# TensorE in written order through the mixing stage of two transformer blocks

## The chip, the core and the metric

The kernel runs on one core of a Trainium2 chip. The metric is the time of one execution on the device, in microseconds (us). TensorE multiplies matrices, VectorE (DVE in the profile) and ScalarE (ACT) work elementwise, GpSimd (POOL) does a few elementwise steps, and SyncE (SP) issues the transfers of the weights. Each engine takes its instructions from a queue of its own, one after the other, and waits at the head of that queue until what the instruction needs is there.

## The reference, cut to what matters

The reference runs two transformer blocks one after the other on 256 tokens with 2,048 features, all in float32. The change lies in the second block, ahead of its feed-forward part:

```
h = rms_norm(x);  z = h @ w_in                       # 1024 pool columns, 3 x 1024 for r, k, v, and 288 more
d = causal_multiscale_pool(z_pool)                   # windows 2, 4, 8, 16
pool_out = einsum('btgc,gcd->btgd', d, pool_w) * pool_scale
w, a, g = small products of the 288 columns, through tanh and sigmoid
kk = k * k_k / norm per head;  k = k * (1 + (a - 1) * k_a)
for t in range(256):                                 # 16 heads of 64, state S of 64 x 64 per head
    S = S * decay_t + (S @ -kk_t) (kk_t a_t)^T + v_t k_t^T;   y_t = S @ r_t
y = group norm of y per head + (sum of r k r_k) v;  y = y * g
x = x + concat(pool_out, y) @ w_out
```

The kernel computes the loop over t in four chunks of 64 tokens. Inside a chunk the steps become small matrix products and the inverse of a triangular 64 x 64 matrix per head; from chunk to chunk the state S is handed on.

## The kernel before, in words

**Fill: the large products.** A weight matrix is streamed from memory in tiles of 128 x 1024 numbers. `load_w` (line 320) has SyncE issue the transfer (L322), ScalarE round the tile to a high part (L325) and VectorE subtract it to get a low part (L326); raw, high and low tiles have three buffers each. `wide_steps` (line 360) multiplies with the weight as the stationary side: each step is a pair of products, L379 over 512 columns and L381 over 256, and 32 pairs fill one PSUM tile `pp` of 256 features; then a copy on ScalarE (L387) and two VectorE instructions (L388, L390) take the sums out. Sixteen products use up one weight tile. `group_steps` (line 337) has the activations as the stationary side: each step is a triple of products over 512 columns (L351 to L353), and twelve products use up one weight tile. `pp` has two buffers. Both are generators: `wide_steps` yields 1 for a pair and `group_steps` 2 for a triple.

**Steps: the small products of the recurrence.** The 16 heads go in two halves of four tiles (two heads in a tile). For each half: `rwkv_pre` (line 1099) squares k, sums it per head (L1084), takes a reciprocal root on VectorE, spreads it (L1090), builds decayed copies of r, k and kk on ScalarE, VectorE and GpSimd, multiplies them (L1161), masks the products on VectorE (L1162, L1163) and transposes a decayed copy (L1169), two tiles at a time. `inverse16` (line 689) inverts the 16 x 16 blocks: SyncE sends the products to memory and back (L701, L702), VectorE does 15 steps of two instructions (L707, L709), GpSimd one copy, and SyncE sends the result out and back again (L710, L712, L716). `rwkv_values` (L1181 to L1188) lays out v. `inverse64` (line 720) starts on GpSimd (L726) and makes the full inverse by products L735, L742 and L744 with VectorE between them. `rwkv_chunk` (line 1206) runs four times per half: L1210, a copy on ScalarE, L1215 and L1217, a copy on ScalarE, L1225 and L1227, an addition on VectorE to the state that the next chunk reads. `rwkv_post` (line 1234) is the group norm: L1240, L1084 and L1090 again. All these products go to PSUM tiles `ps`, of which there are four.

**What sets the order.** The program is written as one sequence. `run` (line 1332) takes a generator of steps, and after each step pulls as many units of fill as the next entry of the list `after` (line 1321) says; the fill is, in this order, the projections of r and v for the first half, the first half of the pool, k, r and v for the second half, the mixing products of the first pool half, the second pool half, the rows of `w_out` for the first half of the heads, and the mixing products of the second pool half. `need` finishes a projection whatever the entries say. The loop is

```
    for half in range(2):
        pre = [None] * 4
        run(merge(rwkv_pre(half, pre), post() if half else ()))
        run(rwkv_half(half, pre))
    run(rwkv_post(1))
    pull(1000)
```

The program is then scheduled as a whole (`schedule_with_timeline_sim=True`, line 1449): for each engine a scheduler plays a timeline forward and, whenever the engine is free in it, takes of the instructions that are ready in it the one that was written first. So an instruction that isn't ready in that timeline is overtaken by later ones; on the chip the order so found is fixed. Lines 1051 to 1057 (small products of the 288 columns) are written ahead of the loop.

**Ten stretches.** Both orders pass through the same steps, so the stage is cut here by steps, and the fill products of each stretch are counted. "Before" is counted in the trace; "written" follows from the list and the loops (a pair is 2 products, a triple 3, and the last step of a PSUM tile counts 1).

| | from the end of ... | to ... | entries of `after` in it | before: pairs' + triples' products | written |
|---|---|---|---|---|---|
| A | first sums, L1084 | last L1161, half 0 | 43 left of r, then 2, 28, 0, 2, 0, 2, 2, 17, 0 | 223 + 0 | 192 + 0 |
| B | A | first L735 | 2, 0, 2, 25, 2, 4, 3, 3, 43 | 214 + 0 | 168 + 0 |
| C | B | first L1210 | 17, 10, 15, 2, 0 | 32 + 0 | 88 + 0 |
| D | C | last L1227 | 4, 2, 3, 2, 3, 3, 0, 0, 3, 10, 3, 2, 3, 2 | 198 + 0 | 80 + 0 |
| E | D | first L1161, half 1 | 4, 1, 0, 28, 24, 3, 13, 1, 21 | 61 + 0 | 190 + 0 |
| F | E | last L1161 | 4, 2, 0, 2, 2, 17, 2 | 8 + 48 | 24 + 27 |
| G | F | first L735 of half 1 | 2, 0, 4, 19, 3, 3, 1, 1, 45 | 128 + 53 | 70 + 69 |
| H | G | first L1210 of half 1 | 15, 10, 13, 1, 0 | 0 + 44 | 58 + 15 |
| I | H | last L1227 of half 1 | 7, 3, 1, 4, 2, 0, 4, 2, 4, 2, 3, 2, 2, 3 | 16 + 143 | 0 + 63 |
| J | I | the rows of `w_out` for the second half | 3, 0, 23, 16, 1, and the rest | 0 | 16 + 114 |

Of the kernel before, what the change touches and what calls it, by code (L numbers as in the profile page):

```python
# [96 lines left out]
def rounds(gens):  # L97

    gens = list(gens)
    while gens:  # L100
        got = [(g, next(g, gens)) for g in gens]
        got = [(g, n) for g, n in got if n is not gens]
        gens = [g for g, n in got]
        yield sum(n or 0 for g, n in got)


def merge(a, b):

    a, b = iter(a), iter(b)
    for _ in a:  # L110
        yield True
        if next(b, False):
            yield True
    yield from b
# [8 lines left out]
def two_blocks_kernel(ctx: ExitStack, tc: tile.TileContext, I: dict, out: bass.AP):  # L123
# [29 lines left out]
    def c(name, lo=0, hi=128):  # L153
        return tabs[name][lo:hi]
# [4 lines left out]
    def prm(name, i, lo=0, hi=128, n=1):  # L159
        t, o = PROW[name]  # L160
        return PT[t][lo:hi, o + i:o + i + n]
# [23 lines left out]
    def wk(tag, F, dt=F32, bufs=2, p=128):  # L185
        return tm(tag, F, dt, bufs, p, quad)

    def psum(F=512, p=128):
        shape = [p] + (list(F) if isinstance(F, (tuple, list)) else [F])
        return ps.tile(shape, F32, tag="ps", name=nm("ps"))  # L190
# [47 lines left out]
    def rsqrt(dst, src, t):  # L238

        ts(out=t.bitcast(I32), in0=src.bitcast(I32), scalar1=1, scalar2=None, op0=ALU.logical_shift_right)  # L240
        ts(out=dst.bitcast(I32), in0=t.bitcast(I32), scalar1=-1, scalar2=0x5F3759DF, op0=ALU.mult, op1=ALU.add)
        for f in (3.0, 12.0, 768.0):
            tt(out=t, in0=dst, in1=dst, op=ALU.mult)
            tt(out=t, in0=t, in1=src, op=ALU.mult)
            stt(dst, t, -f, dst, ALU.add, ALU.mult)
        ts(out=dst, in0=dst, scalar1=-1.0 / 8192, scalar2=None, op0=ALU.mult)

    def tiny(shape):
        return tm("tiny", shape, bufs=8)
# [149 lines left out]
    class Fill:  # L399
# [8 lines left out]
        def pull(self, n):  # L408
            self.owed += n
            while self.todo and self.owed > 0:  # L410
                got = next(self.todo[0], None)
                if got is None:
                    self.todo.pop(0)
                else:
                    self.owed -= got
            if not self.todo:
                self.owed = 0.0
# [11 lines left out]
                self.pull(n)  # L429

    fills = Fill()

    def split(hi, lo, src):
        act(hi, src, AF.Copy)
        tt(out=lo, in0=src, in1=hi.bitcast(F32), op=ALU.subtract)
# [637 lines left out]
    def need(j, half):  # L1073

        for _ in rkvs[j, half]:
            pass
# [3 lines left out]
    def head_sums(p, m, src):  # L1080

        for i in range(2):
            o = 4 * m + 2 * i
            mm(p[:, o:o + 2], src[:, i * 128:(i + 1) * 128], two, start=(m == i == 0), stop=True, skip_group_check=True)  # L1084

    def head_spread(p, f, start=True):

        for i in range(2):
            for j, s in enumerate((LO, HI)):
                mm(p[s, i * 128:(i + 1) * 128], f[:, 2 * i + j:2 * i + j + 1].to_broadcast([128, 64]), ident,  # L1090
                   start=(start and i == 0), stop=True, skip_group_check=True)
# [7 lines left out]
    def rwkv_pre(half, pre):  # L1099

        hs = range(4 * half, 4 * half + 4)

        need(1, half)
        sq = [wk("GB", (4, 128), bufs=4).rearrange("p a b -> p (a b)")[:, :T] for _ in hs]
        for m, h in enumerate(hs):
            act(sq[m], rkv[1, half, m], AF.Square, scale=prm("k_k_2", h))
        yield True
        p = psum()
        for m in range(4):
            head_sums(p, m, sq[m])  # L1110
        n, rn = tiny(16), tiny(16)
        ts(out=n, in0=p[:, :16], scalar1=1e-24, scalar2=None, op0=ALU.max)
        rsqrt(rn, n, tiny(16))
        yield True
        need(0, half)
        for m in (0, 2):
            sp = psum((2, T))
            for i in range(2):
                head_spread(sp[:, i], rn[:, 4 * (m + i):4 * (m + i) + 4], start=(i == 0))
            for _ in rounds([rwkv_pre1(half, m + i, sp[:, i], pre) for i in range(2)]):  # L1120
                yield True
# [53 lines left out]
    def rwkv_values(half, m, SV):  # L1175

        r, k, v = (rkv[j, half, m] for j in range(3))
        t = tm("cva", T, bufs=3)
        stt(t, r, prm("r_k_2", 4 * half + m), k, ALU.mult, ALU.mult)
        pb = psum()  # L1180
        mm(pb[:, :T], c("bones"), t, start=True, stop=True)  # L1181

        pv = psum((4, 128))
        nc.tensor.transpose(pv[:, 1], v[:, 0:128], ident)
        nc.tensor.transpose(pv[:, 2], v[:, 64:192], ident)
        nc.tensor.transpose(pv[:, 3], v[:, 128:256], ident)
        mm(pv[64:128, 0, 0:64], v[0:64, 0:64], ident[0:64, 0:64], start=False, stop=True, skip_group_check=True)
        mm(pv[0:64, 0, 64:128], v[64:128, 192:256], ident[64:128, 64:128], start=False, stop=True, skip_group_check=True)  # L1188
        SV[m] = S = wk("SV", (4, 2, 64), bufs=4)
        act(S[HI, :, 0], pv[HI, :, 0:64], AF.Copy)  # L1190
        act(S[LO, 0:3, 1], pv[LO, 1:4, 64:128], AF.Copy)
        act(S[LO, 3, 1], pv[LO, 0, 64:128], AF.Copy)
        nc.gpsimd.memset(S[LO, 0, 0], 0.0)
        nc.gpsimd.memset(S[HI, 0, 1], 0.0)
        tt(out=v, in0=v, in1=pb[:, :T], op=ALU.mult)
        yield True

    def rwkv_inverse(m, pre, Z):

        GB = pre[2]  # L1200
        X, pd = yield from inverse64([GB[:, i] for i in range(4)], Z[:, m], ("X", "BK")[m % 2])
        for s in (LO, HI):
            tt(out=GB[s, :, s], in0=X[s, :, 1], in1=pd[s, :, 1], op=ALU.subtract)
        yield
# [29 lines left out]
    def rwkv_post(half):  # L1234
        hs = range(4 * half, 4 * half + 4)

        sq = [wk("BT", (4, 128), bufs=4).rearrange("p a b -> p (a b)")[:, :T] for _ in hs]
        for m, h in enumerate(hs):
            pm = psum()
            mm(pm[:, :T], c("bones"), sw[h], start=True, stop=True)  # L1240
            stt(sw[h], pm[:, :T], -1.0 / 64, sw[h], ALU.mult, ALU.add)
            act(sq[m], sw[h], AF.Square)
        yield True
        p = psum()
        for m in range(4):
            head_sums(p, m, sq[m])
        n, rn = tiny(16), tiny(16)
        ts(out=n, in0=p[:, :16], scalar1=1.0 / 64, scalar2=64e-5, op0=ALU.mult, op1=ALU.add)
        rsqrt(rn, n, tiny(16))
        yield True  # L1250
        for m, h in enumerate(hs):
            y = sw[h]
            if m % 2 == 0:
                sp = psum((2, T))
                for i in range(2):
                    head_spread(sp[:, i], rn[:, 4 * (m + i):4 * (m + i) + 4], start=(i == 0))
            stt(y, y, prm("gn_g_2", h), sp[:, m % 2], ALU.mult, ALU.mult)
            stt(y, y, prm("gn_b_2", h), rkv[2, half, m], ALU.add, ALU.add)
            tt(out=y, in0=y, in1=gg[h], op=ALU.mult)
            rwh.append(wk(f"aa{h}", T, F32R, bufs=1))  # L1260
            rwl.append(wk(f"gg{h}", T, F32R, bufs=1))
            split(rwh[h], rwl[h], y)
        yield True

    def rwkv_half(half, pre):

        Z = inverse16([p[2] for p in pre], 4)
        yield True
        SV = [None] * 4
        for m in range(4):  # L1270
            need(2, half)
            yield from rwkv_values(half, m, SV)
        for _ in rounds([rwkv_inverse(m, pre[m], Z) for m in range(4)]):
            yield True
        for j in range(4):
            for _ in rounds([rwkv_chunk(j, pre[m], SV[m], sw[4 * half + m]) for m in range(4)]):
                yield True
# [54 lines left out]
    def run(steps):  # L1332
        for _ in steps:
            pull(next(after))

    def post():
        yield from rwkv_post(0)
        fill.insert(max(1, len(fill) - 1), residual_steps(I["w_out_2"][0], 8, list(zip(rwh[:4], rwl[:4]))))

    for half in range(2):  # L1340
        pre = [None] * 4
        run(merge(rwkv_pre(half, pre), post() if half else ()))
        run(rwkv_half(half, pre))
    run(rwkv_post(1))
    pull(1000)
    n5 = Norm(lambda k: prm("mlp_norm_2", k))
    residual(I["w_out_2"][0], 12, list(zip(rwh[4:], rwl[4:])), n5)
    r5 = spread(n5.finish())
# [104 lines left out]
```

## Time and profile before

| | |
|---|---|
| time, median of 3 runs | 2849.91 us (2837.38 to 2856.08) |
| the profiled execution: its time; its span | 2833.93 us; 2832.2 us |
| TensorE, VectorE, ScalarE, GpSimd busy in the span | 2767.0, 1856.2, 1397.8, 159.2 us |
| mean granted TensorE clock | 0.985 |
| the ten stretches A to J | 1595.85 to 1976.00 us of the span, 380.15 us |
| in them, TensorE busy; VectorE busy | 354.25; 292.26 us |

Times in the profile count from the start of the span. [...] The busy time of TensorE has modelled ends, so that a row of busy time can hide gaps of less than 0.15 us. Counts of a stretch include an instruction that crosses its edge.

### The profile page before, as it was taken

How to read it: one execution, taken by the hardware profiler on the slowest of the kernel's cores; microseconds unless marked ns; L12 is line 12 of the kernel's file. 1: busy time of each engine (PE TensorE's matmuls, PEld its weight loads, DVE VectorE, ACT ScalarE, POOL GpSimd, SP SyncE). 2: the span in 40 equal slices, each digit the busy share in tenths (PEclk: the TensorE clock that was granted, in tenths of full speed). 3: DMA queues.
4: the chain of work that ended last, by engine and by line, in shares of the span. 5: the costliest groups of instructions: out<-in, count | busy, mean ns of one | idle time of the engine just before them, and what ended most of it. 6: DMA issues, size and time to landing. Idle time of an engine off the chain costs nothing.

```text
span 2832.2 us, 40520 instructions
## 1 busy us (share of the span) xinstructions
PE 2767.0 (98%) x15538; PEld 2329.3 (82%) x15538; DVE 1856.2 (66%) x2908; ACT 1397.8 (49%) x2088; POOL 159.2 (6%) x217
## 2 busy tenths in 40 slices
PE   9999989999999999999999999899999999999997
PEld 7888877888888888888887777777888888888886
DVE  7786766555577755775666696876765655656565
ACT  6664545444455544554455544334543444434454
POOL 0003200000000000000001120230000000000001
PEclk9999999999999999999999999899999999999999
DMA  7565644666566656655656363253566666666554
GB/s 218 165 177 150 173 137 119 185 187 186 186 186 189 191 189 188 187 187 190 203 188 183 101 159 108 77 142 105 176 192 193 187 191 191 188 193 204 186 186 149
DMA packets 398200, 487.94 MB, mean 172 GB/s; under 512 B 38426, under 2 KB 283173, under 8 KB 398005
## 3 DMA queue, kind: packets, MB, share of 16 engines
q1 hardware_dynamic: 397221, 482.93, 56.5%
q8 instruction: 122, 2.00, 0.3%
q10 hardware_dynamic: 608, 2.11, 0.2%
q0 software_dynamic: 176, 0.30, 0.1%
q14 instruction: 73, 0.60, 0.1%
HBM read 479.25 MB, written 6.03 MB: 171 GB/s over the span
## 4 chain that ended last, share of the span: by engine, by line
PE 91%; DVE 4%; DMA 2%; ACT 1%; issue 1%; POOL 1%; SPq 0%; DVEq 0%; POOLq 0%; ACTq 0%
PE pp L379 28%; PE pp L381 15%; PE pp L351 14%; PE pp L352 14%; PE pp L353 14%; DVE lo L326 1%; PE ps L267 1%; DMA Z<-s 0%; PE ps L742 0%; DMA raw<-in_w_down_dram 0%; PE ps L1215 0%; PE ps L735 0%; DVE L L1149 0%; PE ps L1217 0%; POOL X L726 0%
## 5 line engine op out<-in xcount | busy, mean ns | idle before, releaser
L326 DVE TENSOR_TENSOR lo<-raw,hi 128x1024 fp32r<-128x1024 f32 x902 | 1108.7, 1229 | 808.0 <-ACT hi L325 784.1
L325 ACT ACTIVATE hi<-raw 128x1024 fp32r<-128x1024 f32 x902 | 953.6, 1057 | 1195.1 <-PE pp L352 554.1
L379 PE MATMUL pp<-xhl,hi 128*128 128x512 f32 x3648 | 1291.7, 397 | 2.1 <-DVE z L388 2.1
L381 PE MATMUL pp<-xhl,lo 128*128 128x256 f32 x3648 | 1030.9, 283 | 2.3 <-DVE lo L326 2.3
L379 PEld LDWEIGHTS pp<-xhl,hi 128*128 128x128 f32 x3648 | 684.0, 188 | 164.7 <-DVE z L388 2.4
L381 PEld LDWEIGHTS pp<-xhl,lo 128*128 128x128 f32 x3648 | 688.8, 189 | 10.2 <-issue 4.7
L353 PE MATMUL pp<-lo,hid 128*128 128x512 f32 x864 | 338.2, 391 | 0.5 <-DVE lo L326 0.5
L351 PE MATMUL pp<-hi,hid 128*128 128x512 f32 x864 | 338.3, 392 | 0.0
L352 PE MATMUL pp<-hi,hid 128*128 128x512 f32 x864 | 337.6, 391 | 0.0
L353 PE MATMUL pp<-lo,xhl 128*128 128x512 f32 (+1 forms) x544 | 206.4, 379 | 0.0
L352 PE MATMUL pp<-hi,xhl 128*128 128x512 f32 (+1 forms) x544 | 206.3, 379 | 0.0
L351 PE MATMUL pp<-hi,xhl 128*128 128x512 f32 (+1 forms) x544 | 206.2, 379 | 0.0
L353 PEld LDWEIGHTS pp<-lo,hid 128*128 128x128 f32 x864 | 162.3, 188 | 35.9 <-DVE lo L326 1.0
L351 PEld LDWEIGHTS pp<-hi,hid 128*128 128x128 f32 x864 | 162.3, 188 | 35.1 <-ACT hi L325 0.3
L352 PEld LDWEIGHTS pp<-hi,hid 128*128 128x128 f32 x864 | 162.4, 188 | 34.3
L351 PEld LDWEIGHTS pp<-hi,xhl 128*128 128x128 f32 x544 | 102.6, 189 | 18.7
L352 PEld LDWEIGHTS pp<-hi,xhl 128*128 128x128 f32 x544 | 102.6, 189 | 18.4
L353 PEld LDWEIGHTS pp<-lo,xhl 128*128 128x128 f32 x544 | 102.5, 188 | 18.3
L933 DVE TENSOR_TENSOR x<-x,pp 128x512 f32<-128x512 f32 x96 | 61.6, 683 | 31.7 <-PE pp L353 31.7
L388 DVE TENSOR_TENSOR z<-pp,z 128x512 f32<-128x512 f32 (+2 forms) x119 | 80.8, 679 | 1.3 <-ACT z L387 1.1
L390 DVE TENSOR_TENSOR z<-z,rstd 128x512 f32<-128x512 f32 x114 | 78.4, 688 | 3.3
L287 POOL TENSOR_TENSOR junk<-x,rows 128x512 f32<-128x512 f32 x8 | 13.4, 1670 | 1110.2 <-ACT junk L284 1110.2
(415 smaller groups left out, 2535.7 us busy)
## 6 DMA issues: line engine op xcount, KB each, us to landing
raw<-in_w_in_dram SPq DMA_DIRECT2D x244, 512.0 KB, 3.6
raw<-in_w_up_dram SPq DMA_DIRECT2D x176, 512.0 KB, 4.4
raw<-in_w_ffn_up_dram SPq DMA_DIRECT2D x128, 512.0 KB, 3.7
raw<-in_w_ffn_down_dram SPq DMA_DIRECT2D x128, 512.0 KB, 4.1
raw<-in_w_down_dram SPq DMA_DIRECT2D x88, 512.0 KB, 3.7
raw<-in_w_out_dram SPq DMA_DIRECT2D x64, 512.0 KB, 3.7
raw<-in_w_ple_gate_dram SPq DMA_DIRECT2D x32, 512.0 KB, 3.9
raw<-in_w_branch_a_dram SPq DMA_DIRECT2D x16, 512.0 KB, 3.7
```

Of the source, the lines that this page charges most:

```text
L267: nc.tensor.transpose(p[:w, m - m0, i * 128:(i + 1) * 128], src[:, i, 128 * m:128 * m + w], ident)
L287: nc.gpsimd.tensor_tensor(out=y, in0=s, in1=self.w2[j], op=ALU.mult)
L325: act(h, r, AF.Copy)
L326: tt(out=l, in0=r, in1=h.bitcast(F32), op=ALU.subtract)
L351: mm(p, xh, h[:, j], start=(k == 0), stop=False, skip_group_check=True)
L352: mm(p, xl, h[:, j], start=False, stop=False, skip_group_check=True)
L353: mm(p, xh, l[:, j], start=False, stop=last, skip_group_check=True)
L379: mm(P[:w, m].rearrange("p a b -> p (a b)"), h[:, j, f], x2.rearrange("p a b -> p (a b)"), start=(k == 0), stop=False, skip_group_check=True)
L381: mm(P[:w, m, 0], l[:, j, f], x2[:, 0], start=False, stop=last, skip_group_check=True)
L388: tt(out=z, in0=P[:w, :nw, 0], in1=z, op=ALU.add)
L390: tt(out=z, in0=z, in1=r()[:w].unsqueeze(1).to_broadcast([w, nw, T]), op=ALU.mult)
L933: tt(out=s, in0=s, in1=p, op=ALU.add)
```

## The change

Both the loop over the halves and the two lines behind it are put into a block in which TensorE's instructions keep the order in which they are written. The order of the other engines and of the transfers is still the scheduler's, which now finds it against that order of TensorE. No instruction is added or taken away.

```
+    def pe_in_order():
+
+        return tc.manual_schedule(engines={mybir.EngineType.PE})
...
-    for half in range(2):
-        pre = [None] * 4
-        run(merge(rwkv_pre(half, pre), post() if half else ()))
-        run(rwkv_half(half, pre))
-    run(rwkv_post(1))
-    pull(1000)
+    with pe_in_order():
+        for half in range(2):
+            pre = [None] * 4
+            run(merge(rwkv_pre(half, pre), post() if half else ()))
+            run(rwkv_half(half, pre))
+        run(rwkv_post(1))
+        pull(1000)
```

## Rows read from the trace of the kernel before

**Rows 1.** The page, part 1: busy time, share of the span, instructions.

```profile
PE 2767.0 (98%) x15538; PEld 2329.3 (82%) x15538; DVE 1856.2 (66%) x2908; ACT 1397.8 (49%) x2088; POOL 159.2 (6%) x217
```

**Rows 2.** Stretches: length, busy (count) of PE, PEld, DVE, ACT, POOL; clock, DMA, GB/s.

```profile
1595.85:1655.30 59.45, 53.48 (x329) 45.25 (x328) 53.22 (x83) 22.58 (x33) 22.07 (x34) 0.94 0.46 130
1655.30:1698.48 43.18, 43.18 (x259) 37.18 (x258) 39.09 (x84) 25.29 (x46) 9.89 (x17) 1.00 0.66 166
1698.48:1717.68 19.20, 17.11 (x352) 14.79 (x352) 14.13 (x22) 3.66 (x4) 4.17 (x5) 1.00 0.36 112
1717.68:1775.51 57.83, 57.83 (x506) 45.68 (x502) 32.58 (x71) 30.24 (x85) 2.02 (x6) 1.00 0.37 106
1775.51:1799.57 24.06, 22.64 (x154) 19.71 (x150) 18.11 (x50) 7.05 (x16) 6.81 (x12) 0.86 0.25 78
1799.57:1837.40 37.83, 29.87 (x145) 24.37 (x146) 37.10 (x63) 14.72 (x24) 11.06 (x18) 0.73 0.25 77
1837.40:1879.21 41.81, 40.76 (x226) 33.67 (x226) 35.68 (x73) 17.46 (x29) 6.39 (x8) 1.00 0.68 172
1879.21:1905.69 26.48, 24.17 (x364) 19.93 (x364) 18.28 (x38) 7.60 (x11) 14.88 (x27) 0.87 0.33 108
1905.69:1964.82 59.13, 57.95 (x472) 43.40 (x468) 37.33 (x79) 30.10 (x86) 0.00 (x0) 1.00 0.40 123
1964.82:1976.00 11.18, 7.26 (x52) 6.62 (x52) 6.73 (x24) 1.28 (x5) 0.00 (x0) 0.61 0.16 47
```

**Rows 3.** The same ten stretches, TensorE's instructions on tile pp alone.

```profile
1595.85:1655.30 59.45, 43.30 (x223) 0.94 0.46 130
1655.30:1698.48 43.18, 39.69 (x214) 1.00 0.66 166
1698.48:1717.68 19.20, 6.67 (x32) 1.00 0.36 112
1717.68:1775.51 57.83, 38.61 (x198) 1.00 0.37 106
1775.51:1799.57 24.06, 14.77 (x61) 0.86 0.25 78
1799.57:1837.40 37.83, 17.15 (x56) 0.73 0.25 77
1837.40:1879.21 41.81, 36.65 (x181) 1.00 0.68 172
1879.21:1905.69 26.48, 12.93 (x44) 0.87 0.33 108
1905.69:1964.82 59.13, 39.38 (x159) 1.00 0.40 123
1964.82:1976.00 11.18, 0.00 (x0) 0.61 0.16 47
```

**Rows 4.** Tile pp on TensorE ahead of the first L1051 product.

```profile
1545.30:1555.19 9.89, 9.89 (x57) 1.00 0.80 248
```

**Rows 5.** Busy time in three spells at the lower clock.

```profile
1646.35:1653.17 6.82, 5.75 (x18) 4.73 (x19) 6.71 (x9) 0.86 (x1) 3.12 (x9) 0.50 0.52 142
1782.88:1789.71 6.83, 6.83 (x25) 6.06 (x25) 4.39 (x23) 0.63 (x1) 0.00 (x0) 0.50 0.23 79
1803.36:1823.84 20.48, 15.79 (x68) 12.93 (x67) 20.16 (x34) 7.08 (x15) 4.55 (x5) 0.50 0.34 104
```

**Rows 6.** TensorE's timeline: start, length, instruction, idle before it and what ended it.

```profile
1702.61 0.68 PE L735 MATMUL ps<-BK,GB 64*64 64x64 f32 x16 [0.72 <-POOL pool L1295]
```

**Rows 7.** Groups by line on VectorE, stretch D: busy us, mean ns, idle before.

```profile
L326 DVE TENSOR_TENSOR lo<-raw,hi 128x1024 fp32r<-128x1024 f32 x13 | 15.9, 1226 | 21.9 <-ACT hi L325 21.7
...
L388 DVE TENSOR_TENSOR z<-pp,z 128x512 f32<-128x512 f32 x4 | 2.8, 692 | 0.1
...
L390 DVE TENSOR_TENSOR z<-z,rstd 128x512 f32<-128x512 f32 x3 | 2.1, 692 | 0.1
```

**Rows 8.** Timeline of SyncE's queue, stretch B: start, length, what it issued.

```profile
1665.59 21.87 SPq L322 DMA_DIRECT2D raw<-in_w_in_dram  x7
```

## The prediction

> **What bounds the kernel now.** I read the page's busy times first: TensorE is busy in 98% of the span, VectorE in 66% [rows 1]. The change touches one part of the span, so I cut that part into the ten stretches of the table above and read each engine's busy time [rows 2]. The reader is to see two kinds of stretch. In A, E, F and J TensorE is idle for 6.0, 1.4, 8.0 and 3.9 us (length less busy), and in A and F VectorE is busy in 90% and 98%: VectorE's work on the steps holds TensorE there. In B, D and I TensorE is full. Together the ten have 380.15 us with TensorE busy in 354.25, so 25.9 us idle. Next I read the granted clock, the column behind POOL: it is 0.94 in A, 0.86 in E, 0.73 in F, 0.87 in H, 0.61 in J and 1.00 elsewhere. [...] Last I counted the fill [rows 3]: that is what the change moves.
>
> **What the change does, part by part.** It takes nothing away; it moves fill products, and with them the splits (L325, L326) and weight transfers that they ask for. Written less before, in products: A -31, B -46, C +56, D -118, E +129, F +16 of pairs and -21 of triples, G -58 and +16, H +58 and -29, I -16 and -80, J +16 and +114. The sum is about nil (+6). So the written order spares fill in the waits of the first half and in both chunk loops and spends it in E and J, where TensorE starves.
>
> The prices: a pair's product takes 39.69/214 = 0.185 us, a triple's 39.38/159 = 0.248 in B and I [rows 3]. In D the fill cost VectorE 15.9 + 2.8 + 2.1 = 20.8 us [rows 7] for 198 products, so 0.105 us each. A stretch then takes what TensorE has to do in it, or what the chain of its steps needs, whichever is longer.
>
> *A and B together* (102.6 us): TensorE's work falls from 96.7 busy by 77 x 0.185 = 14.2 and the 2.9 lost, to 79.6. VectorE is busy 92.3 of 102.6 and the steps' chain runs through it, so VectorE sets the end. With 77 products less it has 8.1 us less to do. Below: all 8.1 come off, 94.5. Above: the split stands ahead of the mask or product of a step just as now, nothing comes off, 102.6. I take the middle, 98.6 (-4.0), since neither row is nearer. TensorE then idles 19 us instead of 6: ahead of L1169, L1161 and L735 there is now less to cover the wait.
>
> *C*: +56 x 0.185 = 10.4 on 17.1 busy; the 2.1 idle stay, they are GpSimd's pace on the four L726 [rows 6]. 29.6 (+10.4).
>
> *D*: 57.8 - 118 x 0.185 = 36.0, and holds. 80 products leave five splits (one per 16) of 1.23 us [rows 7], each of which can stand in front of a step's VectorE or ScalarE part while TensorE waits: nothing to 6.2 us, I take 4, since two entries of the list are 0 and most others 2 to 4 units, less than a split. 40.0 (-17.8).
>
> *E and F together* (61.9): TensorE 52.5 busy less 11.3 lost at the low clock, plus 129 x 0.185 + 16 x 0.185 - 21 x 0.248 = 21.7, is 62.9. VectorE: 55.2 + 124 x 0.105 = 68.2, and that is below. Above: F stays as it is, 37.8, and E is TensorE's 22.6 - 3.4 + 23.9 = 43.1, together 80.9. I take 71.5 (+9.6), nearer to VectorE's sum, because the group norm of the first half and the copies of the first two tiles move under E's fill, which is work that F's full VectorE now does.
>
> *G* (41.8): TensorE 40.8 - 6.7 = 34.1; the chain (masks, three round trips through memory, 30 short VectorE instructions) is above as long as now, and below shorter by VectorE's share of 42 products, 4.4. I take 39.6 (-2.2). *H*: 24.2 + 10.7 - 7.2 - 2.8 + 2.3 idle = 27.2 (+0.7). *I*: 57.95 - 3.0 - 19.8 = 35.2, and holds as in D: 39.2 (-19.9). *J*: 7.3 - 2.4 + 28.3 + 3.0 = 36.2, with no hold, since 130 products stand between its steps, where none does now (+25.0).
>
> Sum: -4.0 + 10.4 - 17.8 + 9.6 - 2.2 + 0.7 - 19.9 + 25.0 = +1.8.
>
> *The clock in the new holds.* All 19.4 lost were taken out above. In the new order TensorE idles some 19 us in A and B, 9 in E and F, 5 in G, 8 in D and I. Below nothing is lost, where the chain and not TensorE sets the end; above as much as now, 19.4. I take 6: one spell's 2.9 on the products of the chain itself in A, and the same in F. In C, gaps of 0.64 to 0.73 us brought the clock no lower [rows 2, 6]. [...]
>
> *Queues.* TensorE waits at its queue's head, so each hold stops the fill behind it, and fill not multiplied frees no weight buffers: SyncE's next transfer waits, and with it a transfer of `inverse16` queued behind. Seven weight transfers went out in 21.87 us of B [rows 8], one in 3.1; that is the most one such wait adds to B and to G. I take nothing, as the chain there is timed without it, and leave 3.1 twice to the upper end. GpSimd keeps its work; it is busy in at most 56% of a stretch (H).
>
> So +1.8 + 6 = +7.8 on the profiled execution's 2833.93 us (1.7 more than its span): 2841.7. That execution lies 16.0 under the median of the runs shown, 2849.91; put on the median, 2857.7, and I say **2858**. Lower ends: -8.1 + 10.4 - 21.8 + 6.3 - 4.4 + 0.7 - 23.9 + 25.0 = -15.8. Upper ends: 0 + 10.4 - 15.6 + 19.0 + 0 + 0.7 - 17.7 + 25.0 + 19.4 + 6.2 = +47.4.
>
> **The rivals.** *VectorE's queue does not get lighter (slower).* The splits run ahead of TensorE by up to three buffers, so fewer products in A, F and G need not bring one mask forward. Then A and B, E and F, and G sit at their upper ends: 4.0 + 9.4 + 2.2 more, and the clock costs as much as now, 13.4 more: 2858 + 29 = 2887. For it: VectorE is at 90% and 98% in A and F. Against: TensorE's place in the order is what releases the buffers. It decides once TensorE's idle time in A to J passes about 60 us.
>
> *The holds vanish (faster).* All chains at their lower ends and the clock full: 2850 - 16 = 2834. For it: 130 products under J's bare chain and 190 in E. Against: A and B lose their cover, as said.
>
> *The clock falls in the chunk loops.* In D and I fill is 67% of TensorE's busy time now, and would be 80 x 0.185 + 63 x 0.248 = 30.4 of 71 us, 43%. If the small products with their short holds let spells at the low clock cover 36 us there, half of that is lost, 18: 2876. Against: small products alone, in C with 6.67 us of fill in 17.11, kept 1.00; for it: a spell in E began without idle time, in a run of small products [rows 5].
>
> *The block also fences its entry.* If no product of the block may go ahead of those of L1051 to L1057, the 9.89 us of fill before the first of them [rows 4] no longer cover that wait: 2868. If on the other hand the scheduler's order were the written one already, nothing would move; the counts of [rows 3] exclude that.
>
> **How the numbers follow.** About 1% (28 us) is what a measurement of this kernel can tell from no change. Forecast (no change, 2846 to 2873) 0.52; VectorE's queue 0.18; holds vanish 0.13; clock in the chunk loops 0.08; fence 0.09. Slower by over 1%, above 2878: most of the first rival and a third of the last two, 0.20; faster, under 2821, only beyond every lower end: 0.03; within 0.77. The range runs from the second rival's 2834 to just short of the first's, 2884.
>
> **What would show it.** In the changed kernel's trace the counts on `pp` by stretch are the table's. Right: D and I shrink to about 40 us with under 7 us idle each; J has no idle; E and F together take 68 to 75 us; A and B 95 to 102 with 15 us idle or more. Wrong: idle of over 10 us in D or I; A and B longer than 103; VectorE idle in F while TensorE waits (then a queue order and not its work holds it); a low clock in D or I.

## The result, and the profile after

The changed kernel takes 2855.64 us in the median of 20 runs (2850.87 to 2878.69). The kernel before, run beside it, takes 2838.22 us in the median of 20 (2834.97 to 2856.71). The ratio is 1.0052, with a 95% interval of 1.0035 to 1.0068: about 15 us slower (the medians lie 17.4 apart), inside the one per cent that was called no change. The forecast's own step was +7.8 us, half of that.

The profiled execution took 2850.87 us, the shortest of the 20; its span is 2849.0 us. The page's first row shows the same work as before [rows 1]:

```profile
PE 2766.3 (97%) x15538; PEld 2329.7 (82%) x15538; DVE 1856.4 (65%) x2908; ACT 1396.7 (49%) x2088; POOL 156.9 (6%) x217
```

The lines of the changed kernel behind the edit are four further down: L1090 of before is L1094, L735 is L739, L1314 is L1318. The ten stretches A to J, cut at the same steps as before [rows 2], with the same columns (the granted clock is a share of full speed; in these stretches of both traces it is 1.00 or 0.50 at any moment, and a figure between is a mean):

```profile
1593.98:1654.39 60.41, 51.25 (x299) 43.67 (x298) 52.56 (x82) 20.21 (x30) 21.64 (x34) 0.85 0.40 114
1654.39:1691.93 37.54, 36.28 (x213) 30.94 (x213) 28.56 (x67) 20.83 (x38) 4.48 (x6) 0.97 0.57 141
1691.93:1725.69 33.76, 30.04 (x409) 25.76 (x409) 23.51 (x40) 9.12 (x13) 9.21 (x16) 0.90 0.45 129
1725.69:1763.31 37.62, 36.19 (x386) 27.12 (x385) 18.57 (x52) 18.81 (x70) 0.52 (x3) 0.95 0.25 71
1763.31:1814.41 51.10, 44.16 (x282) 38.46 (x278) 41.87 (x87) 22.56 (x41) 12.04 (x17) 0.93 0.31 91
1814.41:1848.29 33.88, 24.89 (x141) 19.64 (x140) 30.37 (x46) 10.43 (x16) 10.35 (x16) 0.80 0.36 113
1848.29:1887.48 39.19, 34.36 (x185) 28.03 (x184) 30.53 (x64) 15.85 (x26) 2.81 (x3) 0.97 0.63 161
1887.48:1917.78 30.30, 27.29 (x393) 23.37 (x394) 16.61 (x31) 7.12 (x10) 11.49 (x23) 0.92 0.31 99
1917.78:1955.31 37.53, 36.43 (x372) 26.15 (x368) 21.97 (x64) 18.02 (x70) 3.51 (x10) 0.95 0.19 59
1955.31:1995.20 39.89, 36.84 (x190) 29.81 (x187) 29.27 (x58) 16.96 (x28) 0.00 (x0) 0.96 0.42 131
```

The reader is to see three things. First, the lengths moved as the fill did: D, the chunk loop of the first half, lost 20.2 us and I lost 21.6; C gained 14.6, J 28.7, and E with F 23.1. Together A to J went from 380.15 to 401.22 us, +21.1; the part ahead ends 1.9 us earlier and the one behind is 2.4 shorter, which leaves the span's +16.8. Second, the work did not grow, the waiting did: length less busy, summed over the ten, is 43.5 us of TensorE idle against 25.9, so +17.6. TensorE's busy time for the same products is up by 3.5 (357.72 against 354.25), and the spells at the lower granted clock, 0.50, are 64.8 us long in place of 49.8. Third, of the new idle time E and F together hold the most, 6.5 us (15.9 against 9.4); G holds 3.8, A 3.2, and B, C and D 4.3 between them.

What TensorE waits for in E and F of the kernel before (us in total, times, longest):

```profile
PE pp L352 <- DVE dhl L1314: 4.2, 2, 3.3
PE ps L1161 <- DVE BK L1152: 3.8, 2, 2.3
PE ps L1169 <- ACT BT L1171: 1.0, 1, 1.0
PE pp L379 <- DVE z L388: 0.4, 1, 0.4
```

And in those of the changed kernel:

```profile
PE ps L1094 <- DVE tiny L246: 6.9, 1, 6.9
PE pp L352 <- DVE dhl L1318: 6.6, 1, 6.6
PE pp L351 <- ACT dhl L1317: 2.3, 1, 2.3
```

The first is a spread product, the 32 of the first half's group norm, which stand in the written order ahead of fill and wait for a reciprocal root. The other two are fill itself: the rows of `w_out` for the first pool half, which wait for their operand. Why the reciprocal root is late is in VectorE's timeline (start, length, instruction):

```profile
1788.60 0.17 DVE L1252 TENSOR_SCALAR tiny<-ps 128x16 f32<-128x16 f32 x1 [1.51 <-PE ps L1088]
...
1791.66 0.87 DVE L1141 SCALAR_TENSOR_TENSOR sw<-rk,PT,ps 128x256 f32<-128x256 f32 x2
...
1792.96 2.96 DVE L1153 TENSOR_TENSOR L<-sw,E 64x256 f32<-64x256 f32 x4
...
1802.25 0.16 DVE L246 TENSOR_SCALAR tiny<-tiny 128x16 f32<-128x16 f32 x1
```

L1252 begins the root and L246 ends it: thirteen instructions of 0.17 us each where nothing slows them, that took 13.8 us from first to last because the copies of the heads (L1141, L1153 and on, 6.9 us), two splits and an L388 stand between them in VectorE's queue.

### The profile page after: what moved, and what is told of

It reads as the page before. It is cut to its first block, busy times and chain, and to the rows that moved or that the text cites. A ratio compares the mean times of both kernels' runs of the same rounds, so it can differ in the third digit from the quotient of the medians.

```text
span 2849.0 us, 40536 instructions
## 1 busy us (share of the span) xinstructions
PE 2766.3 (97%) x15538; PEld 2329.7 (82%) x15538; DVE 1856.4 (65%) x2908; ACT 1396.7 (49%) x2088; POOL 156.9 (6%) x217
## 5 line engine op out<-in xcount | busy, mean ns | idle before, releaser
L326 DVE TENSOR_TENSOR lo<-raw,hi 128x1024 fp32r<-128x1024 f32 x902 | 1110.4, 1231 | 810.7 <-ACT hi L325 791.3
L390 DVE TENSOR_TENSOR z<-z,rstd 128x512 f32<-128x512 f32 x114 | 80.7, 708 | 3.2
L388 DVE TENSOR_TENSOR z<-pp,z 128x512 f32<-128x512 f32 (+2 forms) x119 | 80.7, 678 | 1.1 <-ACT z L387 1.1
```

Source lines behind the costliest of these rows:

```text
L326: tt(out=l, in0=r, in1=h.bitcast(F32), op=ALU.subtract)
L388: tt(out=z, in0=P[:w, :nw, 0], in1=z, op=ALU.add)
L390: tt(out=z, in0=z, in1=r()[:w].unsqueeze(1).to_broadcast([w, nw, T]), op=ALU.mult)
```

## The experiments

Three readings were put against each other first. *Q*: the two waits above, each a matter of what stands where in VectorE's queue, are the loss. *V*: VectorE's list as a whole sets the end of E and F. *C*: the loss is in the first half, where C grew by 14.6. Ratios below are to the kernel before, run on the same chip; the changed kernel's own is 1.0052 [1.0035, 1.0068].

**1. The written order in the first half alone.**

```
-    with pe_in_order():
-        for half in range(2):
...
+    with pe_in_order():
+        half_steps(0)
+    half_steps(1)
+    run(rwkv_post(1))
+    pull(1000)
```

> Only the first half (stretches A to D) is in the written order; the second half and the rest are the scheduler's. Theory Q (the order of VectorE's queue holds TensorE at two places behind the first half: before the 32 spread products in E, 6.9 us, and before the triple products of pool_mix(0) in F, 2.3 + 6.6 us, and 2.8 us before those of pool_mix(1) in J): those places go back to the scheduler, which puts other products there, so 2834 to 2842 us, ratio to the kernel before 0.998 to 1.002. Rival V (VectorE's sum of work in E and F sets the end, and the written order leaves more of it there): the fill left over is spent as before, 2838 to 2846. Rival C (the loss is the 14.6 us that C grew, in the first half): 2850 to 2856, ratio 1.004 to 1.006.

(`half_steps` is the body of the loop.) Measured: 2846.75 us, 1.0038 [1.0015, 1.0062].

**2. In the second half and the rest alone** (`half_steps(0)` ahead of the block, everything else in it).

> Only what follows the first half (E to J) is in the written order. By the scheduler's order the first half spends more fill, so less is left for E to J. Theory Q: the holds in E, F and J are there, and less fill to lay before them: 2850 to 2860 us, ratio 1.004 to 1.008. Rival V: 2845 to 2855. Rival C: the loss is in the first half, so 2836 to 2842, ratio 0.999 to 1.001.

Measured: 2845.40 us, 1.0021 [1.0003, 1.0039]. Each part costs, 0.38% and 0.21%, and together they make about the whole. Q's figure fits neither run, since it put no loss in the first half; C's nearly fits the first, but leaves no loss for the second, whose interval lies above 1. V's times come nearest: the first run is 0.75 us above its range, the second inside.

In the first half of the changed kernel the loss is not C's growth alone. D gave up its 118 products at nearly their price (21.8 us at 0.185 each; it is 20.2 shorter), and C took 14.6 us for 56 (10.4). The largest part is A: with 31 products less (5.7 us) it is no shorter (60.41 against 59.45), and VectorE is busy in 52.56 us of it as it was in 53.22. B gave up 46 (8.5 us) and is 5.6 shorter. That VectorE's queue is what keeps A from getting shorter is argued, not shown.

**3. More fill ahead of the late spread** (one line of `after`: three entries).

```
-            ... 4, 1, 0, 28, 24, 3, 13, 1, 21, 4, ...
+            ... 4, 1, 0, 28, 24, 3, 34, 0, 1, 4, ...
```

> The changed kernel with three entries of the list moved: 13, 1, 21 in E become 34, 0, 1, so that 21 more units of fill (42 products, 7.8 us) stand in TensorE's order ahead of the 32 spread products L1094 and behind the 16 of the first two heads. Theory Q: the hold of 6.9 us shrinks below 1.5 us and E is 5 to 7 us shorter: 2847 to 2851 us, ratio to the kernel before 1.003 to 1.005 where the changed kernel has 1.0052. Rival V: VectorE has the same work and its end does not move: the hold turns up at the next reader (L1165 behind BK, or in F), and the time stays at 2853 to 2858. Rival C: the same as V here.

Measured: 2851.90 us, 1.0052 [1.0030, 1.0073], no different from the changed kernel. The waits in E and F:

```profile
PE pp L352 <- DVE dhl L1318: 8.0, 1, 8.0
PE pp L351 <- ACT dhl L1317: 3.5, 1, 3.5
PE pp L381 <- DVE lo L326: 2.7, 2, 2.5
PE pp L379 <- DVE z L388: 1.3, 1, 1.3
```

The hold of 6.9 us is gone, as Q said, and its time is back at the others: E and F take 84.0 us where they took 85.0, with 15.6 us idle where there were 15.9. A hold that goes without shortening its stretch was not the limit.

**4. The pool mixing cut in two**, so that 128 products lie between what makes the operand and what reads it.

```
-    fill = [..., rkvs[0, 1], rkvs[2, 1], pool_mix(0), pool_proj(1), pool_mix(1)]
+    fill = [..., rkvs[0, 1], pool_mix(0), rkvs[2, 1], pool_out(0), pool_proj(1), pool_mix(1), pool_out(1)]
```

> The changed kernel with pool_mix cut in two, its pool products and its residual rows (pool_out), and the list of fill in another order: pool_mix(0) stands ahead of rkvs[2, 1], pool_out(0) behind it; pool_out(1) behind the residual rows of the first half. The 128 products of rkvs[2, 1] now lie between the pool products of 0 and the triple products that read their result. Theory Q: the holds of 2.3 and 6.6 us in F and of 2.8 us in J go: 2843 to 2848 us, ratio 1.001 to 1.003. Rival V: 2853 to 2858, the idle time moves to other lines of E to G. Rival C: 2852 to 2858.

(`pool_out` is the part of `pool_mix` that multiplies with the rows of `w_out`.) Measured: 2874.24 us, 1.0129 [1.0101, 1.0158], slower than anything expected. In E and F both waits for `dhl` are gone, but the wait ahead of L1094 is 9.7 us where it was 6.9, and L1165 waits 3.0: the two stretches take 84.3 us. The loss lies later, where the cut put the pool products of the second half right behind the projection that makes their operand (G and H of this run, 87.0 us where the changed kernel has 69.5):

```profile
PE pp L379 <- DVE dhl L439: 11.4, 2, 8.7
```

No execution of this kernel had a mean granted clock above 0.980, so the wait need not be all of the loss. It moved a second thing beside the one meant; only its E and F are used below.

**Where VectorE's list begins.** After these, E and F were cut once more, at the first spread product of the second half: ahead of it VectorE can't begin on the heads, behind it it can. Length, then busy time of TensorE, its weight loads, VectorE, ScalarE, GpSimd; the kernel before:

```profile
1775.58:1790.53 14.95, 14.95 (x79) 13.37 (x78) 9.85 (x36) 5.04 (x13) 0.00 (x0) 0.77 0.27 89
1790.53:1837.40 46.87, 37.49 (x218) 30.64 (x218) 45.32 (x75) 16.67 (x28) 17.87 (x30) 0.78 0.24 74
```

The changed kernel:

```profile
1763.38:1789.64 26.26, 26.26 (x160) 23.23 (x160) 17.56 (x39) 13.40 (x25) 1.68 (x3) 1.00 0.47 133
1789.64:1848.36 58.72, 42.79 (x259) 34.87 (x258) 54.72 (x93) 19.52 (x33) 20.69 (x30) 0.83 0.27 85
```

Ahead of the spread VectorE idles 8.7 us while TensorE works off fill; behind it VectorE is busy in 93% and TensorE idles 15.9. That gave theory *S*: in E the written order lays its fill in series with VectorE's list, ahead of it and not beside it. But the run of experiment 1, which has E and F in the scheduler's order with nearly the same fill (232 products on `pp` where the changed kernel has 243), shows the same ahead of the spread:

```profile
1762.91:1789.36 26.45, 26.45 (x161) 23.40 (x160) 17.32 (x40) 13.28 (x25) 1.68 (x3) 1.00 0.45 135
1789.36:1841.42 52.06, 39.79 (x248) 32.01 (x247) 50.95 (x87) 18.28 (x32) 20.54 (x30) 0.87 0.27 85
```

VectorE idles 9.1 us ahead of it there too. The two stretches take 78.5 us, 16.7 more than before; so of the 23.1 by which they grew, at most 6.5 are left for their own order, all of it behind the spread, and the rest comes with the fill that the first half's order leaves to them.

**5. The spread earlier.** 27 of the 55 units of fill ahead of it go behind it, and the rest of `rkvs[0, 1]` is asked for one step later.

```
-        need(0, half)
         for m in (0, 2):
...
+        need(0, half)
         r = rkv[0, half, m]
...
-            ... 0, 28, 24, 3, 13, 1, 21, 4, ...
+            ... 0, 2, 16, 10, 40, 1, 21, 4, ...
```

(In the first half the request stays where it was.)

> The changed kernel with the first spread products of the second half, L1094 of heads 0 and 1, written earlier: 27 of the 55 units of fill (52 products) that stood ahead of them now stand behind, and the rest of rkvs[0, 1] is asked for one step later. Theory S (serial): in E TensorE first works off 104 fill products for 24 us in which VectorE idles 7.0 us, and then VectorE is busy 44.0 of 47.9 us and holds TensorE; VectorE's list begins with the spread. With the spread some 9 us earlier E and F together are 6 to 9 us shorter than the 85.0 of the changed kernel, both holds shrink: 2843 to 2848 us, ratio to the kernel before 1.001 to 1.003. Rival Q (VectorE's fixed order of instructions, not the moment at which its list begins, makes the two holds): 1 to 2 us, as moving fill in front of the second spread gave: 2850 to 2855. Rival C (the rest of the loss is elsewhere, in C, H, J): same as Q.

Measured: 2848.82 us, 1.0026 [1.0002, 1.0049]. The same two pieces:

```profile
1769.68:1786.59 16.91, 16.91 (x107) 15.05 (x107) 12.94 (x37) 8.81 (x18) 1.79 (x3) 1.00 0.31 94
1786.59:1848.22 61.63, 49.38 (x313) 40.25 (x312) 59.00 (x96) 23.60 (x39) 21.82 (x30) 0.92 0.35 112
```

E and F are 78.5 us, 6.4 less, what S gave. 54 products have changed sides, and the piece behind the spread is only 2.9 us longer for it; VectorE idles 4.0 + 2.6 us instead of 8.7 + 4.0. That holds beyond this one trace: with the spread where it was, E and F take 84.0 to 86.5 us in five traces (the changed kernel, 3, 4, 6 and 7); with the early spread 78.4 to 80.7 in four (5 and 8 to 10).

The time is less clear. It moved the same way (half of the loss), though the intervals of the two ratios overlap. This trace's span is as long as the changed kernel's (2849.1 against 2849.0): what E and F gained was lost ahead of them, 2.9 us of it in D (40.5 us at a granted clock of 0.87) and 1.9 ahead of A. Eight of the twelve executions had a mean granted clock of 0.984 to 0.986 and took 2843 to 2849 us, the other four 0.977 to 0.983 and 2851 to 2869; none of the changed kernel's twenty was above 0.983. Whether the move raised the clock isn't shown.

**6. VectorE's list shorter.** Three VectorE instructions on each tile of the first half are left out, and with them their result.

```
+            if half:
                 stt(y, y, prm("gn_g_2", h), ...)
                 stt(y, y, prm("gn_b_2", h), ...)
                 tt(out=y, in0=y, in1=gg[h], op=ALU.mult)
```

> The changed kernel without the group norm's three VectorE operations on the four tiles of the first half (L1261 to L1263, 12 instructions, 5.3 us of VectorE in E and F); their result is left out of the computation, all else is there. Theory S: VectorE's list sets the end of F, so E and F are 4 to 6 us shorter and the time 2849 to 2852. Rival Q: the 12 stand where VectorE would otherwise wait for others; 0 to 2 us: 2853 to 2856.

Measured: 2854.56 us, 1.0064 [1.0042, 1.0086]. Taking VectorE's work away gained nothing: S's figures (4 to 6 us, 2849 to 2852) are missed, Q's are met. E and F are 84.1 us; the piece behind the spread:

```profile
1790.67:1848.51 57.84, 41.62 (x259) 34.17 (x258) 49.23 (x77) 17.94 (x29) 20.69 (x30) 0.85 0.27 85
```

VectorE does 5.5 us less and idles 8.6 instead of 4.0. Its timeline shows where:

```profile
1811.34 0.69 DVE L326 TENSOR_TENSOR lo<-raw,hi 128x512 fp32r<-128x512 f32 x1 [1.12 <-ACT hi L325]
1814.11 0.69 DVE L326 TENSOR_TENSOR lo<-raw,hi 128x512 fp32r<-128x512 f32 x1 [2.08 <-ACT hi L325]
1815.99 0.68 DVE L1166 TENSOR_TENSOR GB<-ps,C 64x512 f32<-64x512 f32 x1 [1.19 <-PE ps L1165]
```

The next thing for VectorE is the masks L1166, and their products L1165 stand on TensorE behind 44 products of fill. So it looks as if against VectorE's list there is a second limit of nearly the same length, TensorE's own order; the next run tests that.

**7. Of those 44 products 42 moved** to behind the spread products of heads 2 and 3.

```
-            ... 28, 24, 3, 13, 1, 21, 4, 2, 0, 2, 2, 17, ...
+            ... 28, 24, 3, 13, 1, 0, 4, 2, 0, 2, 23, 17, ...
```

> The changed kernel with one group of 21 units of fill (42 products, 8 us) moved within TensorE's order: from between the first group norm's spread products and the pair products L1165 of heads 0 and 1 to behind the spread products of heads 2 and 3. Theory A (alternation): in E and F neither engine's sum sets the end; VectorE waits for TensorE behind fill (before the masks of heads 0 and 1), and TensorE then waits for VectorE (the copies of heads 2 and 3, dhl) with no fill left, since both queues are in a fixed order. Moved, the same 42 products lie beside the copies of heads 2 and 3: E and F together 77 to 81 us where the changed kernel has 85.0, time 2848 to 2853, ratio 1.001 to 1.004. Rival V (VectorE's list is the bound; its sum with the idle time at the start of E makes the 85): 83 to 85, time 2854 to 2857. That leaving out 12 VectorE operations moved nothing speaks for A.

Measured: 2858.03 us, 1.0070 [1.0041, 1.0099]. Theory A (alternation), as I put it, is wrong: E and F are 86.5 us, not 77 to 81; V's 83 to 85 are nearer. The fill that was to cover the copies of heads 2 and 3 stops as well:

```profile
PE pp L379 <- DVE z L388: 7.8, 1, 7.8
```

L388 empties a PSUM tile of the fill and stands in VectorE's queue behind those copies. Fill is not independent of VectorE: after two PSUM tiles it needs it too. VectorE, in the piece behind the spread, is then busy 55.7 of 60.2 us.

**8 to 10. Put together.** Experiments 5 and 7; with them the cut of 4 for the first pool half alone; and with that the residual rows of the first half laid around the pool products of the second (16 of their 32 steps on either side).

```
-            ... 0, 2, 16, 10, 40, 1, 21, 4, 2, 0, 2, 2, 17, ...
+            ... 0, 2, 16, 10, 40, 1, 0, 4, 2, 0, 2, 23, 17, ...
...
+        fill.insert(max(1, len(fill) - 2), islice(rest, 16))
+        fill.insert(len(fill) - 1, rest)
```

> early_spread with the same 21 units moved as well. early_spread had 78.6 us in E and F, with a hold of 6.7 us before the triple products left. Theory A: the two add up, 71 to 75 us in E and F; time 2840 to 2846, ratio 1.000 to 1.002. Rival V: with VectorE's list started early its sum, 72 us, is the end, and moving fill changes the holds' place only: 76 to 79 us, time 2846 to 2850.

> early_late, and pool_mix(0) cut in two, its pool products ahead of rkvs[2, 1] and its residual rows behind it; everything for pool_mix(1) as in the changed kernel. Theory A: the wait for dhl in F (2.4 + 6.7 us in early_spread) goes for good, since the products of rkvs[2, 1] lie between: E and F 69 to 74 us, time 2838 to 2845, ratio 0.999 to 1.002. Rival V: no change beside early_late, the idle time stands before L1165 instead.

> early_late_split, and in J the pool products of pool_mix(1) in the middle of the residual rows of the first half, so that the second half of these rows lies between them and the rows that read their result. Holds of 2.0 + 0.9 us in J go: 2835 to 2842 us, ratio 0.998 to 1.001, about the kernel before. If the wait for the operands of those pool products comes back (it did, with 11.4 us, where all the rows stood behind them), 2843 to 2850.

Measured: 2850.21 us, 1.0049 [1.0025, 1.0072], E and F 80.7; 2860.05 us, 1.0071 [1.0040, 1.0101], E and F 78.4; 2847.14 us, 1.0041 [1.0017, 1.0065], E and F 78.4. None goes more than 0.1 us below experiment 5's 78.5, and in each the longest wait is for L388 (7.7, 6.4 and 6.4 us). That misses theory A's figures (71 to 75 and 69 to 74 us) and is nearer to V's 76 to 79. The third run's time lies in the range that was tied to the return of the wait of 11.4 us, but that wait isn't in its trace. None beats the kernel before.

**11. The spread earlier in both halves.**

```
-        22, 14, 2, 28, ...
+        22, 20, 2, 28, ...
```

> early_spread, and the same in the first half: of the products that stood ahead of the first spread there (86), those of rkvs[0, 0] that are left after 20 units stand behind it. In A VectorE is busy 52.6 of 60.4 us, and idle mostly ahead of its list. Theory S: A is another 3 to 6 us shorter: 2838 to 2844 us, ratio 0.999 to 1.002, about the kernel before. Rival Q and C: no more than 1 us beyond early_spread.

Measured: 2874.88 us (2874.49 without the execution of the trace), 1.0110 [1.0078, 1.0141]; S said 0.999 to 1.002. This is a miss and stays unexplained: its one trace is of an execution at a mean granted clock of 0.649, whose stretches can't be set beside the others. Of its five other executions four had 0.975 to 0.977, where experiment 5's twelve had 0.977 to 0.986; what brought the clock down isn't shown.

**12. The same in the scheduler's order.**

> The kernel before (the scheduler's order) with the same entries and the same later request for rkvs[0, half]. Theory S: the scheduler already moves fill behind the spreads where TensorE would wait, and VectorE's list starts when it can; 2832 to 2842 us, ratio 0.998 to 1.001. Rival Q: the scheduler's order is by its own estimates and the text's order hardly counts: the same 2838. If S holds for the scheduler too and its list starts some 5 us earlier in A and in E: 2828 to 2833.

Measured: 2834.42 us, 0.9989 [0.9968, 1.0011]. With the scheduler's order the place of the spread in the text makes no difference that can be measured.

## Why the prediction was right, and where it was not

**A and B** (-4.0 forecast): 97.95 us, -4.7. The sum came out, its reason only in part, so some of this is luck. VectorE has 11.2 us less to do in the two (8.1 forecast), but nearly all of that in B: in A it does 0.7 less, and A is no shorter. B, 5.6 shorter, is TensorE's, busy in 36.28 us of 37.54. The sign named, at least 15 us of TensorE idle, failed: 10.4, as TensorE was busy 87.5 us where 79.6 were forecast, with the clock in A at 0.85.

**D and I** (-17.8 and -19.9): 37.6 and 37.5 us, -20.2 and -21.6, with 1.4 and 1.1 us idle where 4 each were allowed. The splits did not get into the chunk chain's way.

**G** (-2.2): -2.6; all its idle time, 4.8 us, is the wait of the first L739 for GpSimd's L730, with which it ends. **C** (+10.4): +14.6, 3.7 us idle instead of 2.1 and a spell of 6.83 us at 0.50; the gaps ahead of L739 were now 0.37 to 1.53 us, and my sentence that gaps of 0.64 to 0.73 brought the clock no lower didn't carry over to them (whether they brought the spell on isn't shown). **H** (+0.7): +3.8; TensorE was busy 27.3 us where 24.9 were forecast, with the clock at 0.92 and not full. **J** (+25.0, "no hold"): +28.7, with the hold of its own fill that I had excluded, 2.0 + 0.9 us. The wait that ends G, and the hold in J:

```profile
1887.48 1.12 PE L739 MATMUL ps<-X,GB 64*64 64x64 f32 x16 [4.83 <-POOL X L730]
...
1966.48 0.50 PE L351 MATMUL pp<-hi,dhl 128*128 128x512 f32 x1 [1.96 <-ACT dhl L1317]
1967.86 0.80 PE L352 MATMUL pp<-hi,dhl 128*128 128x512 f32 x1 [0.87 <-DVE dhl L1318]
```

**E and F** (+9.6, and 2.9 more for a spell at the lower clock): +23.1. This is the term that was mis-sized most, and it went past its upper end (80.9 us; measured 85.0). VectorE's work was 4.1 us over its forecast (72.3 against 68.2); the other 9.4 are VectorE's idle time, 12.7 us where 71.5 allowed 3.3. What failed is the reason for laying the sum near VectorE's work, that the group norm and the copies of the first two tiles "move under E's fill". For the copies that isn't so. 120 of the fill products of E stand ahead of the first spread product, and the copies need that product. So VectorE idles 8.7 us ahead of it and 4.0 behind: 72.3 + 12.7 = 85.0. That the idle time ahead lengthens E and F is shown by experiment 5, which took 6.4 us off them by moving fill from before the spread to behind it. It isn't the written order alone that lays the fill there: the scheduler's order did so too in experiment 1. The sign named for a queue order as the cause, VectorE idle in F while TensorE waits, came in small part: 1.7 us in the 20.5 us of F in which TensorE idles 9.0. That removing either late hold by itself gives nothing is shown by 3, 4 and 7, and that removing 5.5 us of VectorE's work gives nothing, by 6. That VectorE's list and TensorE's order in that piece are each about as long as the other is the reading that fits these; whether the two shortened together (6 with 7) would gain was not run.

**The clock** (+6): mis-sized as well. The forecast took out 19.4 us as what the clock cost before (2.9 in A, 11.3 in E and F, 2.8 in H, 2.4 in J) and put 6 us back, in A and F; the rival of the chunk loops has 18. Each of these is half of what TensorE is busy in spells at 0.50 (5.75 us in A, 6.83 in E, 15.79 in F [rows 5]), an estimate: no run shows these terms as time lost. What the trace of the changed kernel shows is the pace of fill at the end of the spell in C: a pair takes 0.64 us in it and 0.34 behind it, 47% less:

```profile
1699.08 0.63 PE L379 MATMUL pp<-xhl,hi 128*128 128x512 f32 x1
...
1699.72 0.63 PE L379 MATMUL pp<-xhl,hi 128*128 128x512 f32 x1
...
1701.41 0.39 PE L379 MATMUL pp<-xhl,hi 128*128 128x512 f32 x1
...
1701.75 0.40 PE L379 MATMUL pp<-xhl,hi 128*128 128x512 f32 x1
```

At half of TensorE's busy time the changed kernel's ten spells (64.8 us, TensorE busy in 46.9) cost 23.5. Not all of that is time, where a chain sets the end; but in C, D, H, I and J, which the forecast had at the full clock, it is by this estimate about 10 us. Four of the spells, in C, D, F and I:

```profile
1694.28:1701.11 6.83, 5.91 (x57) 5.03 (x56) 5.31 (x9) 1.14 (x3) 5.37 (x10) 0.50 0.47 136
1745.48:1748.89 3.41, 3.41 (x22) 2.36 (x21) 2.04 (x5) 1.68 (x4) 0.02 (x1) 0.50 0.02 5
1827.40:1841.05 13.65, 6.93 (x15) 4.68 (x16) 13.43 (x22) 2.92 (x6) 8.50 (x13) 0.50 0.20 66
1919.56:1922.97 3.41, 3.19 (x11) 2.55 (x12) 1.08 (x5) 0.83 (x3) 1.71 (x6) 0.50 0.00 0
```

**The rivals.** *The clock falls in the chunk loops*: no; D and I have one spell of 3.41 us each, a granted clock of 0.95. That is 6.8 us together, beside 1.4 and 1.1 us of idle time, far from the 36 that the rival needed; whether the idle time brought them on isn't shown. *The block fences its entry*: no; the same 57 products of fill still stand ahead of the first L1055 (9.90 us, to 1554.50), and others among L1055 to L1061, 26 of them behind 1579.5 us. *VectorE's queue does not get lighter*: its deciding sign, 60 us of TensorE idle, was not reached (43.5), and B and G got shorter; but A kept its length, as this rival had it, and E and F went past the upper end that it gave them. *The holds vanish*: only in D and I.

So the sign and the class were right by the sum of the ten terms, which was small against most of them. In the trace the ten stretches grew by 21.1 us where the terms and the clock gave 7.8, a miss of 13.3: E and F are 13.5 over their term, C, H and J 11.0 over theirs, the others 5.2 under, and the 6 for the clock takes up part of it. That 2858 lies 2.4 us from the measured 2855.64 is luck: the step was too small by 9.6 us (7.8 against 17.4), and the median of three on which it was put, 2849.91, was 11.7 above the median of twenty, 2838.22.

## What to carry to other kernels

Fill that is to cover an elementwise engine's list must stand behind the product that starts the list; ahead of it, the same fill is in series with it. Here that was worth 6.4 us in E and F; the same move in the first half (11) made the kernel slower, for a reason that stayed open. When a bound is a sum of one engine's work over a stretch, ask at which product that work may begin, and add the time before it. And take a hold for the limit of its stretch only after the stretch gets shorter without it: two holds here, of 6.9 and 9.0 us, came back under other names when they were covered.

## What the runs showed of the hardware

Many of VectorE's splits that ran beside a GpSimd instruction took longer than the others. Of the changed kernel's 79 splits L326 on 1024 columns between 1590 and 2000 us, the 64 that overlap no GpSimd instruction took at most 1.23 us; of the 15 that overlap one, six took no more than that and nine took 1.55 to 2.21. In E one took 2.08 us, where the mean in D of before is 1.23 [rows 7], and L243 on 16 columns took 0.60 where it took 0.17 at 1789.85 us. The run of experiment 6 has the same pair, a split of 2.08 us at 1800.68 beside L1170 at 1800.64. VectorE:

```profile
1792.44 0.60 DVE L243 TENSOR_TENSOR tiny<-tiny 128x16 f32<-128x16 f32 x1
...
1799.65 2.08 DVE L326 TENSOR_TENSOR lo<-raw,hi 128x1024 fp32r<-128x1024 f32 x1
```

GpSimd:

```profile
1792.28 0.73 POOL L1149 TENSOR_TENSOR aa<-sw,aa 128x256 f32<-128x256 f32 x1 [18.79 <-DVE sw L1141]
...
1799.61 1.04 POOL L1170 TENSOR_TENSOR X<-BK,PC 128x512 f32<-128x512 f32 x1 [0.20 <-DVE BK L1156]
```

No run here took GpSimd's instructions away, so what made these longer isn't shown. In E and F the 15 splits average 1.33 us.
